# Odd layer's attention: the copies of transposed maps ahead of the exponentials, and low parts one step later

## The chip, the cores and the metric

The kernel runs on one core of a Trainium2 chip, as one launch. The metric is the device time of that launch in microseconds; three runs of the kernel before gave 1513.31, 1510.46 and 1513.28, a median of 1513.28. An engine here is one of five instruction streams that run side by side and wait for each other by semaphores: PE (TensorE: matmuls and transposes), DVE (VectorE), ACT (ScalarE), POOL (GpSimd) and SP (here only an issuer of DMAs). Each works through its own list strictly in order. Matmul results lie in PSUM, in banks of 512 f32 per partition; everything else lies in SBUF.

## The reference, cut

One inference step of a trunk with two layers over 128 context tokens (one group) and 256 latent tokens (the other), model width 1024. Each layer is: half SwiGLU, a mixer, half SwiGLU, each behind an RMS norm and an adaptive shift, scale and gate. The mixer of the even layer is differential attention beside a short convolution; that of the odd layer, which this change is about, is attention with 16 query heads on 4 key heads of 64, a window of 128 on either side among latent tokens, all context keys, and one sink logit per head:

```python
def _odd_mixer(h, w_in, w_out, qk_g, sink, rope=None, kv_ctx=None):
    q, k, v = jnp.split(h @ w_in, [...], axis=-1)
    q, k = _rms_norm(q, qk_g[0]), _rms_norm(k, qk_g[1])
    if kv_ctx is None:                  # context tokens: read context only
        o = _dense_sink_attention(q, k, v, sink)
    else:                               # latent tokens: window + cached context
        o = _window_sink_attention(_rope(q), _rope(k), v, k_ctx, v_ctx, sink)
    return o.reshape(b, s, ODD_OUT) @ w_out

# per block of 128 queries:
s_c = einsum("bqgrd,bcgd->bgrqc", qi, k_ctx) * scale
s_l = where(valid, einsum("bqgrd,bkgd->bgrqk", qi, ks) * scale, -inf)
p = softmax(concatenate([s_c, s_l, sink_column]))[..., :-1]
o = einsum(p[context], v_ctx) + einsum(p[window], vs)
```

## The kernel before, in words

**Products.** Large matrix products are done in f32 by parts: each operand is split into a rounded high part and the low part that is left, and a product is three matmuls, xh·wh + xl·wh + xh·wl (lines 178 to 180, names `proj`, `down`). Weights come by DMA (`raw`, on SP's queue), ACT writes their high part `wh` (line 80), and the DVE or POOL the low part `wl` (line 84). `refill_half` does half a weight tile of that at the end of each attention step.

**Steps.** The odd layer's attention is 24 steps (u, c, i): key head u of 4, chunk c of 2 (two query heads each), and i, a block of 128 queries: i = 0 the context block with 128 keys, i = 1 and 2 the two latent blocks with 384 keys. A step handles two heads, p = 0 and 1. `pipeline` runs the steps interleaved. In its round s it does, in this order of writing, which is the order of each engine's list:

- a(s), `scores`: PE multiplies queries and keys into two PSUM tiles `s` (line 1214) and, for i > 0, adds the mask by a matmul (1221). The DVE takes the maxima of both heads (1227, `omx`), multiplies them by the queries' scale (1229), forms the negative bias (1231, `ong`) and the sink's exponent (1235, `oes`). ACT computes the exponentials `e` of both heads with their sums (1239) and of the sink (1243).
- m(s-1), `normalised`: the DVE adds the sink to the sum (1247), takes the reciprocal (1248), and POOL multiplies both heads' maps by it (1249).
- fill(s): other work beside the attention. In the first half of the steps it is a piece of the query projection of a later head (PE, lines 178 to 180), with its norm (691 to 708, rsqrt on POOL at 189) and rotary embedding (718 to 722, DVE); from step 18 on, pieces of the output projection (`down`).
- b(s-3), `transposed`: PE transposes each map `e` in blocks of 128 into a PSUM tile `aT` (1259), and ACT copies that to SBUF as `at_sb` (1261).
- c(s-4), `attend`: PE multiplies the transposed maps with the values into the PSUM tile `oo` (1272). After i = 2 a chunk is finished: ACT writes its high part `gh` (1279), the DVE its low part `gl` (1280); they are the operands of the output projection.

So three rounds lie between a map's scores and its transposes, and four between scores and products.

**Buffers.** The PSUM tiles `aT`, `oo` and the running projection share four banks (tag "mm"); score tiles, norm rows and some small tiles share four others (tag "at"). A new tile takes the bank that was taken longest ago, and its first matmul waits until the last reader of the old tile is done. `at_sb` and two rotary temporaries share four SBUF buffers; maps have five.

The even layer's mixer uses `pipeline` as well, with its own functions.

Of the kernel before, what the change touches and what calls it, by code (L numbers as in the profile page):

```python
# [8 lines left out]
F32 = mybir.dt.float32  # L9
# [3 lines left out]
ALU = mybir.AluOpType  # L13
# [5 lines left out]
T = 384  # L19
# [39 lines left out]
class Weights:  # L59
# [82 lines left out]
    def refill(self):  # L142
        self.split(self.np + self.SPLIT)
# [10 lines left out]
class Kernel:  # L154
# [640 lines left out]
            nc.tensor.transpose(tp[:, h * P:(h + 1) * P], self.ck[:, h * P:(h + 1) * P], self.ident)  # L795
        nc.scalar.activation(out, tp[:, 0:n * P].rearrange("p (h t) -> p h t", h=n), AF.Copy)

    def pipeline(self, n, a, m, b, c, lag, fill, refill):

        for s in range(n + lag + 1):  # L800
            if s < n:
                a(s)
            if 0 <= s - 1 < n:
                m(s - 1)
            fill(s)
            if 0 <= s - lag < n:
                b(s - lag)
            if 0 <= s - lag - 1 < n:
                c(s - lag - 1)
            refill()  # L810
# [282 lines left out]
    def odd_mixer(self, l):  # L1093
        nc = self.nc
        okt = self.mix.tile([P, 4, 512], F32, tag="kt", name="okt")
        kt = [okt[:, i] for i in range(4)]
        vt = [self.mix.tile([P, 512], F32, tag=f"v{i}", name=f"ov{i}")[:, 0:256] for i in range(3)] + [self.cv]
# [4 lines left out]
        qs, rq = {}, {}  # L1102
# [83 lines left out]
        gs = [self.g_tiles(), self.g_tiles()]  # L1186
# [8 lines left out]
                next(out[0][2], None)  # L1195

        out, order = [], list(range(KC))
        self.pipeline(*self.odd_attention(qs, rq, kt, vt, gs), 3, fill, self.w.refill_half)
        self.out_projection(out[0], gs, order, self.mod_need(l, 5), (l, 2))

    def odd_attention(self, qs, rq, kt, vt, gs):

        nc = self.nc
        steps = [(u, c, i) for u in range(4) for c in range(2) for i in range(3)]

        def scores(u, c, i):

            keys = [kt[u // 2 + (0 if p == u % 2 else 2)] for p in range(2)]
            s = [self.ps("at", "s"), self.ps("at", "s")]
            n = 128 if i == 0 else 384  # L1210
            k0 = 384 if i == 0 else 0
            for p in range(2):
                hs = slice(64 * p, 64 * p + 64)
                nc.tensor.matmul(
                    s[p][:, 0:n], qs[u][hs, c, i * P:(i + 1) * P], keys[p][hs, k0:k0 + n],
                    start=True, stop=(i == 0),
                )
            if i:
                m0 = 256 if i == 1 else 128
                for p in range(2):  # L1220
                    nc.tensor.matmul(
                        s[p][:, m0:m0 + P], self.ident16, self.masks[i - 1], start=False, stop=True
                    )
            scale = rq[u][:, i, c]
            mx = self.small(2, "omx")
            for p in range(2):
                nc.vector.tensor_reduce(out=mx[:, p:p + 1], in_=s[p][:, 0:n], axis=AX.X, op=ALU.max)
            h0 = 4 * u + 2 * c
            nc.vector.tensor_tensor(out=mx, in0=mx, in1=scale, op=ALU.mult)
            ng = self.small(2, "ong")  # L1230
            nc.vector.scalar_tensor_tensor(
                out=ng, in0=mx, scalar=-1.0, in1=self.negsink[:, h0:h0 + 2], op0=ALU.mult, op1=ALU.min
            )
            es = self.small(2, "oes")
            nc.vector.tensor_tensor(out=es, in0=ng, in1=self.negsink[:, h0:h0 + 2], op=ALU.subtract)
            e = self.b3("e")
            rs = self.small(2, "ors")
            for p in range(2):
                nc.scalar.activation(
                    e[:, p, 0:n], s[p][:, 0:n], AF.Exp, bias=ng[:, p:p + 1], scale=scale[:, p:p + 1],  # L1240
                    accum_out=rs[:, p:p + 1],
                )
            nc.scalar.activation(es, es, AF.Exp)
            return e, n, rs, es

        def normalised(e, n, rs, es):
            nc.vector.tensor_tensor(out=rs, in0=rs, in1=es, op=ALU.add)
            nc.vector.reciprocal(rs, rs)
            nc.gpsimd.tensor_tensor(
                out=e[:, :, 0:n], in0=e[:, :, 0:n], in1=rs.unsqueeze(2).to_broadcast([P, 2, n]), op=ALU.mult  # L1250
            )
            return e, n

        def transposed(e, n):
            out = []
            for p in range(2):
                tp = self.ps("mm", "aT")
                for b in range(n // P):
                    nc.tensor.transpose(tp[:, b * P:(b + 1) * P], e[:, p, b * P:(b + 1) * P], self.ident)  # L1259
                at = self.a2("at_sb")[:, 0:n]  # L1260
                nc.scalar.activation(at, tp[:, 0:n], AF.Copy)
                out.append(at)
            return out, n

        def attend(u, c, i, ats, n):
            if i == 0:
                self.oo = self.ps("mm", "oo")
            vs = slice(u * HD, (u + 1) * HD)
            v = [vt[0]] if i == 0 else [vt[3], vt[1], vt[2]]
            for b in range(n // P):  # L1270
                for p in range(2):
                    nc.tensor.matmul(  # L1272
                        self.oo[64 * p:64 * p + 64, i * P:(i + 1) * P], v[b][:, vs],
                        ats[p][:, b * P:(b + 1) * P], start=(b == 0), stop=(b == n // P - 1),
                    )
            if i == 2:
                gh, gl = gs[u // 2]
                ch = 2 * (u % 2) + c
                nc.scalar.activation(gh[:, ch], self.oo[:, 0:T], AF.Copy)
                nc.vector.tensor_tensor(  # L1280
                    out=gl[:, ch], in0=self.oo[:, 0:T], in1=gh[:, ch].bitcast(F32), op=ALU.subtract
                )

        maps, ats = {}, {}

        def a(n):
            maps[n] = scores(*steps[n])

        def m(n):
            maps[n] = normalised(*maps[n])  # L1290

        def b(n):
            ats[n] = transposed(*maps.pop(n))

        def c(n):
            attend(*steps[n], *ats.pop(n))

        return len(steps), a, m, b, c


    def setup(self):
# [342 lines left out]
```

## Time and profile before

| | us |
|---|---|
| median of three runs | 1513.28 |
| lowest, highest | 1510.46, 1513.31 |
| the profiled execution | 1516.13 |
| its span in the trace | 1514.3 |
| from the first scores of the odd attention to the first `down` behind its last step | 1105.24 to 1189.94 |
| mean granted clock of TensorE, as a share of full speed | 0.993 |

The profile is of one execution and lists what each engine ran, with the time that it stood idle ahead of each group and the event that ended it. In a row of groups, x24 is the number of instructions; behind the bar stand their busy time in us, the mean of one in ns, and the idle time before them with its releasers. In a timeline, a row is start, duration, engine, line, operation, output <- inputs; the bracket is the idle time before it and its releaser. A window's row has busy times of five engines (with instruction counts), then the granted TensorE clock (PEclk, 1.00 is full), the share of the DMA engines and their rate. PEld is TensorE's weight load, which overlaps its matmuls.

### The profile page before, as it was taken

What the parts mean: (1) busy time and instruction counts of PE and PEld (TensorE: products, weight loads), DVE (VectorE), ACT (ScalarE), POOL (GpSimd) and SP (SyncE); (2) the same over time, 40 slices, a digit from 0 to 9 for tenths busy, and PEclk for the clock granted to TensorE, in tenths of its full rate; (3) what the DMA queues carried; (4) which work ended last, traced back from release to release, by engine and by line L of the source; (5) the groups of instructions that cost most, each with busy time, mean ns of one, the idle gap of its engine ahead of it and who ended that gap; (6) DMA issues with size and microseconds to landing.
All of it is one profiled execution on the core that took longest, in us unless ns stands there. A gap on an engine that the chain in (4) does not pass through costs nothing.

```text
span 1514.3 us, 22676 instructions
## 1 busy us (share of the span) xinstructions
PE 1479.7 (98%) x9082; PEld 1414.8 (93%) x9082; DVE 1047.3 (69%) x1670; ACT 658.1 (43%) x1235; POOL 149.3 (10%) x99
## 2 busy tenths in 40 slices
PE   6999999999999999999999999999998999999998
PEld 6999999999899999999999999999965799999998
DVE  3848799777777887878689777766786485344432
ACT  3633233465555632334464333425666564323322
POOL 1100000015322100000010000000454220000000
PEclk8999999999999999999999999999998999999999
DMA  9846887553323465866546667634330034344322
GB/s 349 279 159 216 253 266 234 181 168 112 112 86 118 145 209 187 256 219 204 157 153 212 215 199 245 218 110 152 114 99 29 5 112 142 109 137 142 110 79 76
DMA packets 192155, 248.61 MB, mean 164 GB/s; under 512 B 5845, under 2 KB 170290, under 8 KB 192050
## 3 DMA queue, kind: packets, MB, share of 16 engines
q1 hardware_dynamic: 190974, 245.79, 49.9%
q8 instruction: 71, 1.16, 0.3%
q10 hardware_dynamic: 1076, 1.38, 0.3%
q14 instruction: 34, 0.28, 0.1%
HBM read 244.26 MB, written 2.36 MB: 163 GB/s over the span
## 4 chain that ended last, share of the span: by engine, by line
PE 80%; DVE 10%; ACT 4%; issue 2%; DMA 2%; POOL 1%; ACTq 0%; DVEq 0%; POOLq 0%
PE proj L178 16%; PE proj L180 16%; PE proj L179 16%; PE down L178 8%; PE down L179 8%; PE down L180 8%; DVE macc L225 3%; DVE wl L84 2%; ACT wh L80 1%; DMA wm<-in_w_mod 1%; DVE acc L342 1%; PE m_sum L237 1%; PE oo L1272 1%; DVE x L347 1%; PE aT L1259 1%
## 5 line engine op out<-in xcount | busy, mean ns | idle before, releaser
L178 PE MATMUL proj<-xh,wh 128*128 128x384 f32 (+1 forms) x1648 | 562.8, 341 | 1.7 <-ACT xh L395 1.7
L180 PE MATMUL proj<-xh,wl 128*128 128x384 f32 (+1 forms) x1648 | 557.2, 338 | 0.9 <-DVE wl L84 0.9
L179 PE MATMUL proj<-xl,wh 128*128 128x384 f32 (+1 forms) x1648 | 556.4, 338 | 0.0
L84 DVE TENSOR_TENSOR wl<-raw,wh 128x1024 fp32r<-128x1024 f32 (+2 forms) x332 | 360.6, 1125 | 187.5 <-ACT wh L80 187.1
L80 ACT ACTIVATE wh<-raw 128x1024 fp32r<-128x1024 f32 x356 | 321.6, 952 | 138.8 <-PE down L179 109.3
L178 PEld LDWEIGHTS proj<-xh,wh 128*128 128x128 f32 x1648 | 310.6, 188 | 14.8 <-issue 6.8
L180 PEld LDWEIGHTS proj<-xh,wl 128*128 128x128 f32 x1648 | 311.1, 189 | 1.2 <-DVE wl L84 1.2
L179 PEld LDWEIGHTS proj<-xl,wh 128*128 128x128 f32 x1648 | 310.6, 188 | 0.0
L178 PE MATMUL down<-gh,wh 128*128 128x384 f32 x832 | 280.6, 337 | 0.4 <-ACT gh L642 0.4
L179 PE MATMUL down<-gl,wh 128*128 128x384 f32 x832 | 278.4, 335 | 0.5 <-DVE gl L643 0.5
L180 PE MATMUL down<-gh,wl 128*128 128x384 f32 x832 | 278.2, 334 | 0.0
L225 DVE SCALAR_TENSOR_TENSOR macc<-wm,cpad,macc 128x1024 f32<-128x1024 f32 x210 | 258.1, 1279 | 3.0 <-DMA wm<-in_w_mod 2.4
L642 ACT ACTIVATE gh<-gf 128x768 fp32r<-128x768 f32 x44 | 37.2, 846 | 291.9 <-DVE gf L632 287.5
L178 PEld LDWEIGHTS down<-gh,wh 128*128 128x128 f32 x832 | 156.3, 188 | 4.4 <-issue 3.6
L179 PEld LDWEIGHTS down<-gl,wh 128*128 128x128 f32 x832 | 156.4, 188 | 1.0 <-DVE gl L643 0.8
L180 PEld LDWEIGHTS down<-gh,wl 128*128 128x128 f32 x832 | 156.3, 188 | 0.0
L625 ACT ACTIVATE sg<-proj 128x384 f32<-128x384 f32 x78 | 37.5, 488 | 136.0 <-PE proj L180 136.0
L347 DVE SCALAR_TENSOR_TENSOR x<-down,m,x 128x128 f32<-128x128 f32 (+1 forms) x160 | 59.1, 411 | 49.5 <-PE down L180 48.7
L632 DVE TENSOR_TENSOR gf<-proj,sg 128x384 f32<-128x384 f32 x78 | 43.2, 554 | 70.2 <-PE proj L180 70.2
L84 POOL TENSOR_TENSOR wl<-raw,wh 128x1024 fp32r<-128x1024 f32 x24 | 61.4, 2560 | 107.3 <-ACT wh L80 95.4
L643 DVE TENSOR_TENSOR gl<-gf,gh 128x768 fp32r<-128x768 f32 x44 | 42.2, 959 | 40.1 <-ACT gh L642 40.1
L189 POOL TENSOR_TENSOR nr<-nv,neghalf 128x3 f32<-128x3 f32 x6 | 5.1, 851 | 570.6 <-DVE nv L415 570.6
(221 smaller groups left out, 1084.9 us busy)
## 6 DMA issues: line engine op xcount, KB each, us to landing
raw<-in_ffn_w SPq DMA_DIRECT2D x85, 1024.0 KB
wm<-in_w_mod SPq DMA_DIRECT2D x126, 512.0 KB
raw<-in_ffn_w SPq DMA_DIRECT2D x32, 768.0 KB
raw<-in_ffn_w SPq DMA_DIRECT2D x32, 640.0 KB
raw<-in_even_w_in SPq DMA_DIRECT2D x12, 1024.0 KB
raw<-in_odd_w_in SPq DMA_DIRECT2D x6, 1024.0 KB
raw<-in_even_w_out SPq DMA_DIRECT2D x4, 1024.0 KB
raw<-in_odd_w_out SPq DMA_DIRECT2D x4, 1024.0 KB
```

What stands on the lines that cost most here:

```text
L80: self.k.nc.scalar.activation(parts[0][:, a:b], raw[:, a:b], AF.Copy)
L84: engine.tensor_tensor(out=lo[:, a:b], in0=raw[:, a:b], in1=h[:, a:b].bitcast(F32), op=ALU.subtract)
L178: mm(out, w[0], x[0], start=first, stop=False)
L179: mm(out, w[0], x[1], start=False, stop=False)
L180: mm(out, w[1], x[0], start=False, stop=last)
L225: nc.vector.scalar_tensor_tensor(out=acc, in0=t, scalar=c, in1=acc, op0=ALU.mult, op1=ALU.add)
L237: self.nc.tensor.matmul(ps[32 * j:32 * j + 32, 0:256], c, v[:, j], start=first, stop=last)
L347: self.nc.vector.scalar_tensor_tensor(out=self.x[oc][:, a:b], in0=psum[:, a:b], scalar=gate[:, oc, g:g + 1], in1=self.x[oc][:, a:b], op0=A ...
L625: nc.scalar.activation(sg[c], out[:, 0:T], AF.Silu)
L632: nc.vector.tensor_tensor(out=gf[:, c], in0=out[:, 0:T], in1=sg[c], op=ALU.mult)
L642: nc.scalar.activation(gh, gf, AF.Copy)
L643: nc.vector.tensor_tensor(out=gl, in0=gf, in1=gh.bitcast(F32), op=ALU.subtract)
```

## The change

`scores` is cut in two: `scores` keeps the matmuls, and a new function `exponentials` has all behind them (maxima, scale, bias, exponentials). `pipeline` gets an optional argument e. With it, a round is: a(s), the score matmuls; b(s-3), transposes and copies; e(s), maxima and exponentials; m(s-1); fill(s); c(s-4); refill. Without it, as in the even layer, the round is what it was. The low part `gl` of a finished chunk is no longer written in `attend` but noted in a list, which `low_parts` works off at the end of the next m; for the last key head (u = 3) at once. Every operation of before is there once, with the same operands.

```diff
@@ -795,15 +795,19 @@
             nc.tensor.transpose(tp[:, h * P:(h + 1) * P], self.ck[:, h * P:(h + 1) * P], self.ident)
         nc.scalar.activation(out, tp[:, 0:n * P].rearrange("p (h t) -> p h t", h=n), AF.Copy)
 
-    def pipeline(self, n, a, m, b, c, lag, fill, refill):
+    def pipeline(self, n, a, m, b, c, lag, fill, refill, e=None):
 
         for s in range(n + lag + 1):
             if s < n:
                 a(s)
+            if e and 0 <= s - lag < n:
+                b(s - lag)
+            if e and s < n:
+                e(s)
             if 0 <= s - 1 < n:
                 m(s - 1)
             fill(s)
-            if 0 <= s - lag < n:
+            if not e and 0 <= s - lag < n:
                 b(s - lag)
             if 0 <= s - lag - 1 < n:
                 c(s - lag - 1)
@@ -1195,7 +1199,8 @@
                 next(out[0][2], None)
 
         out, order = [], list(range(KC))
-        self.pipeline(*self.odd_attention(qs, rq, kt, vt, gs), 3, fill, self.w.refill_half)
+        a, e, m, b, c = self.odd_attention(qs, rq, kt, vt, gs)
+        self.pipeline(24, a, m, b, c, 3, fill, self.w.refill_half, e)
         self.out_projection(out[0], gs, order, self.mod_need(l, 5), (l, 2))
 
     def odd_attention(self, qs, rq, kt, vt, gs):
@@ -1221,6 +1226,9 @@
                     nc.tensor.matmul(
                         s[p][:, m0:m0 + P], self.ident16, self.masks[i - 1], start=False, stop=True
                     )
+            return s, n
+
+        def exponentials(u, c, i, s, n):
             scale = rq[u][:, i, c]
             mx = self.small(2, "omx")
             for p in range(2):
@@ -1277,17 +1285,26 @@
                 gh, gl = gs[u // 2]
                 ch = 2 * (u % 2) + c
                 nc.scalar.activation(gh[:, ch], self.oo[:, 0:T], AF.Copy)
-                nc.vector.tensor_tensor(
-                    out=gl[:, ch], in0=self.oo[:, 0:T], in1=gh[:, ch].bitcast(F32), op=ALU.subtract
-                )
-
-        maps, ats = {}, {}
+                lows.append((gl[:, ch], self.oo[:, 0:T], gh[:, ch].bitcast(F32)))
+                if u == 3:
+                    low_parts()
+
+        def low_parts():
+            for out, psum, high in lows:
+                nc.vector.tensor_tensor(out=out, in0=psum, in1=high, op=ALU.subtract)
+            lows.clear()
+
+        maps, ats, lows = {}, {}, []
 
         def a(n):
             maps[n] = scores(*steps[n])
 
+        def e(n):
+            maps[n] = exponentials(*steps[n], *maps[n])
+
         def m(n):
             maps[n] = normalised(*maps[n])
+            low_parts()
 
         def b(n):
             ats[n] = transposed(*maps.pop(n))
@@ -1295,7 +1312,7 @@
         def c(n):
             attend(*steps[n], *ats.pop(n))
 
-        return len(steps), a, m, b, c
+        return a, e, m, b, c
 
 
     def setup(self):
```

The line numbers of the changed kernel are higher: scores 1219 and 1226, maxima 1235 to 1243, exponentials 1247 and 1251, sum, reciprocal and scaling 1255 to 1257, transposes 1267, copies 1269, products 1280, `gh` 1287, `gl` 1294.

What moves in the engines' lists shows at three places. ACT, rounds 12 and 13, before: `e` are a round's own exponentials, `at_sb` the copies of the round three earlier, `gh` the high part of the chunk finished four rounds earlier.

```order
L1239 ACTIVATE e,ors<-s,ong,orq_10570 128x128 x2
L1243 ACTIVATE oes<-oes 128x2
L1261 ACTIVATE at_sb<-aT 128x128 x2
L1279 ACTIVATE gh<-oo 128x384
L1239 ACTIVATE e,ors<-s,ong,orq_10570 128x384 x2
L1243 ACTIVATE oes<-oes 128x2
L1261 ACTIVATE at_sb<-aT 128x384 x2
```

and now:

```order
L1269 ACTIVATE at_sb<-aT 128x128 x2
L1247 ACTIVATE e,ors<-s,ong,orq_10582 128x128 x2
L1251 ACTIVATE oes<-oes 128x2
L1287 ACTIVATE gh<-oo 128x384
L1269 ACTIVATE at_sb<-aT 128x384 x2
L1247 ACTIVATE e,ors<-s,ong,orq_10582 128x384 x2
L1251 ACTIVATE oes<-oes 128x2
```

The copies of the transposed maps of steps 9 and 10 stood behind the exponentials of steps 12 and 13, and stand ahead of them now; `gh` stays behind the 128-key exponentials.

DVE, the end of round 12 and round 13, before: first sum and reciprocal of step 11, then the low part, the maxima of step 13 and what follows from them, sum and reciprocal of step 12, and the norm of a projection (`orq_v`).

```order
L1247 TENSOR_TENSOR ors<-ors,oes 128x2
L1248 RECIPROCAL ors<-ors 128x2
L1280 TENSOR_TENSOR gl<-oo,gh 128x384
L1227 TENSOR_REDUCE omx<-s 128x1 x2
L1229 TENSOR_TENSOR omx<-omx,orq_10570 128x2
L1231 SCALAR_TENSOR_TENSOR ong<-omx,negsink 128x2
L1235 TENSOR_TENSOR oes<-ong,negsink 128x2
L1247 TENSOR_TENSOR ors<-ors,oes 128x2
L1248 RECIPROCAL ors<-ors 128x2
L708 TENSOR_SCALAR orq_v<-cols 128x12
```

and now:

```order
L1255 TENSOR_TENSOR ors<-ors,oes 128x2
L1256 RECIPROCAL ors<-ors 128x2
L1235 TENSOR_REDUCE omx<-s 128x1 x2
L1237 TENSOR_TENSOR omx<-omx,orq_10582 128x2
L1239 SCALAR_TENSOR_TENSOR ong<-omx,negsink 128x2
L1243 TENSOR_TENSOR oes<-ong,negsink 128x2
L1255 TENSOR_TENSOR ors<-ors,oes 128x2
L1256 RECIPROCAL ors<-ors 128x2
L1294 TENSOR_TENSOR gl<-oo,gh 128x384
L708 TENSOR_SCALAR orq_v<-cols 128x12
```

The low part `gl` went from ahead of the maxima of step 13 to behind the reciprocal of step 12. Nothing else moved.

PE, round 9 (a 128-key step with a projection piece), before: scores of step 9, six projection matmuls, transposes of step 6, products of step 5.

```order
L1214 MATMUL s<-okt,oq 128x128 x2
L178 MATMUL proj<-xh,wh 128x384
L179 MATMUL proj<-xl,wh 128x384
L180 MATMUL proj<-xh,wl 128x384
L178 MATMUL proj<-xh,wh 128x384
L179 MATMUL proj<-xl,wh 128x384
L180 MATMUL proj<-xh,wl 128x384
L1259 MATMUL aT<-con,e 128x128 x2
L1272 MATMUL oo<-at_sb,v_4446 64x128 x2
L1272 MATMUL oo<-at_sb,ov_9815 64x128 x2
L1272 MATMUL oo<-at_sb,ov_9816 64x128 x2
```

and now:

```order
L1219 MATMUL s<-okt,oq 128x128 x2
L1267 MATMUL aT<-con,e 128x128 x2
L178 MATMUL proj<-xh,wh 128x384
L179 MATMUL proj<-xl,wh 128x384
L180 MATMUL proj<-xh,wl 128x384
L178 MATMUL proj<-xh,wh 128x384
L179 MATMUL proj<-xl,wh 128x384
L180 MATMUL proj<-xh,wl 128x384
L1280 MATMUL oo<-at_sb,v_4446 64x128 x2
L1280 MATMUL oo<-at_sb,ov_9815 64x128 x2
L1280 MATMUL oo<-at_sb,ov_9816 64x128 x2
```

The transposes went from behind the fill's matmuls to straight behind the scores; the products stay behind the fill. POOL's list is in the same order as before.

## The prediction

> **What bounds the kernel now.** I read the page first, its span and its busy times.
>
> ```profile
> span 1514.3 us, 22676 instructions
> PE 1479.7 (98%) x9082; PEld 1414.8 (93%) x9082; DVE 1047.3 (69%) x1670; ACT 658.1 (43%) x1235; POOL 149.3 (10%) x99
> ```
>
> The kernel as a whole hangs on TensorE. A reordering on ACT and DVE can win only where PE stands or runs at half clock. So the second view is the table of windows. I cut the odd layer's attention at the score matmuls: seven stretches (steps 0 to 5, then three steps each, the last 21 to 23), then what follows it; the last two rows are chosen for their clock.
>
> ```profile
> core 0: us, PE busy (x) PEld busy (x) DVE busy (x) ACT busy (x) POOL busy (x), PEclk, DMA share, GB/s
> 1105.24:1126.79 21.55, 19.92 (x120) 13.45 (x120) 20.23 (x51) 11.68 (x37) 12.00 (x7) 1.00 0.15 49
> 1126.79:1137.53 10.74, 10.41 (x79) 7.42 (x77) 7.60 (x30) 7.18 (x24) 5.74 (x4) 1.00 0.30 99
> 1137.53:1148.00 10.47, 10.14 (x76) 6.44 (x74) 7.23 (x28) 8.37 (x26) 4.23 (x4) 1.00 0.01 2
> 1148.00:1161.67 13.67, 10.62 (x64) 6.32 (x62) 8.95 (x27) 8.48 (x28) 8.10 (x6) 0.79 0.23 77
> 1161.67:1171.23 9.56, 7.62 (x61) 4.78 (x59) 5.08 (x22) 6.76 (x27) 4.30 (x4) 0.86 0.01 3
> 1171.23:1180.47 9.24, 9.09 (x71) 6.36 (x69) 5.18 (x22) 5.53 (x20) 2.52 (x3) 0.90 0.00 0
> 1180.47:1189.94 9.47, 7.38 (x64) 4.59 (x62) 5.19 (x22) 7.02 (x27) 4.09 (x4) 1.00 0.05 16
> 1189.94:1514.30 324.36, 318.17 (x1856) 315.07 (x1854) 146.70 (x222) 116.50 (x195) 14.66 (x10) 1.00 0.33 106
> 1156.10:1162.40 6.30, 5.40 (x27) 3.44 (x27) 2.50 (x13) 4.23 (x14) 4.38 (x4) 0.50 0.51 166
> 1170.00:1172.90 2.90, 2.90 (x19) 2.34 (x18) 0.77 (x4) 1.72 (x7) 1.07 (x1) 0.50 0.03 6
> ```
>
> Call the seven stretches A to G. In A the DVE is busy for 94%. In B and C PE is busy for 97%. In D, E and G PE stands for 3.05, 1.94 and 2.09. In D to F two pieces run at a granted clock of 0.50. Behind 1189.94 PE is busy for 98%: an earlier end of the attention passes on whole. Third, the groups of the attention alone, with what ended the idle time ahead of each:
>
> ```profile
> L1259 PE MATMUL aT<-con,e 128*128 128x128 f32 x98 | 16.6, 292 | 5.8 <-ACT at_sb L1261 5.3 <-POOL e L1249 0.3
> ...
> L1229 DVE TENSOR_TENSOR omx<-omx,orq 128x2 f32<-128x2 f32 x24 | 11.1, 463 | 0.9
> ...
> L189 POOL TENSOR_TENSOR orq<-orq_v,neghalf 128x12 f32<-128x12 f32 x3 | 7.7, 2574 | 4.1 <-PE s L1214 4.1
> L84 POOL TENSOR_TENSOR wl<-raw,wh 128x1024 fp32r<-128x1024 f32 x3 | 7.1, 2356 | 0.0
> ...
> L1280 DVE TENSOR_TENSOR gl<-oo,gh 128x384 fp32r<-128x384 f32 x6 | 3.3, 558 | 10.0 <-ACT gh L1279 10.0
> ```
>
> L1259 and L1280 are the two waits that the change takes on. PE stands 5.3 us at transposes (aT) that need the bank of a map which ACT has not copied yet (at_sb). The DVE stands 10.0 us at the low parts (gl) until ACT has written gh, six times. The timeline of steps 22 and 23 shows how one leads to the other.
>
> ```profile
> 1183.68 0.92 PE L1214 MATMUL s<-okt,oq 64*128 64x384 f32 x4
> ...
> 1184.32 0.56 DVE L1280 TENSOR_TENSOR gl<-oo,gh 128x384 fp32r<-128x384 f32 x1 [1.97 <-ACT gh L1279]
> ...
> 1184.65 0.82 PE L1259 MATMUL aT<-con,e 128*128 128x128 f32 x6
> 1184.79 1.02 DVE L1227 TENSOR_REDUCE omx<-s 128x1 f32<-128x384 f32 x2
> ...
> 1185.77 0.92 PE L1214 MATMUL s<-okt,oq 64*128 64x384 f32 x4
> ...
> 1186.32 0.67 ACT L1239 ACTIVATE e<-s,ong,orq 128x384 f32<-128x384 f32 x1 [2.04 <-DVE ong L1231]
> 1186.51 0.17 DVE L1248 RECIPROCAL ors<-ors 128x2 f32<-128x2 f32 x1
> ...
> 1186.84 0.61 POOL L1249 TENSOR_TENSOR e<-e,ors 128x256 f32<-128x256 f32 x1 [2.86 <-DVE ors L1248]
> ...
> 1187.73 0.86 ACT L1261 ACTIVATE at_sb<-aT 128x384 f32<-128x384 f32 x2
> ...
> 1188.35 0.85 PE L1259 MATMUL aT<-con,e 128*128 128x128 f32 x6 [1.45 <-ACT at_sb L1261]
> ...
> 1189.94 0.44 PE L178 MATMUL down<-gh,wh 128*128 128x384 f32 x1
> ```
>
> gl holds back the maxima of step 22 to 1184.79, these the exponentials to 1186.32, and behind both exponentials stand the copies of maps that PE had finished by 1185.47: they start at 1187.73. PE, one step on, waits for them until 1188.35. One late gl costs one standing PE.
>
> **The change part by part.** Nothing is added or removed: per step two copies, two exponentials and six transposes stay, and six gl of 0.56 stay. No DMA moves past another; POOL's and SP's queues keep their order.
>
> (1) What PE needs by itself. Step 22 runs without a gap: 1183.68 to 1185.77 is 2.09. Step 23 is its scores (1183.68 to 1184.65, 0.97) and its transposes and products (1188.35 to 1189.94, 1.59): 2.56. A 128-key step has those 1.59 less two thirds of the 0.82 of transposes, and some 0.4 of scores: 1.45, an estimate. Three steps: 6.1.
>
> (2) What ACT needs: its busy 6.76 in E and 7.02 in G.
>
> (3) What DVE and POOL need, now that gl stands behind the reciprocal. From the start of the maxima to the reciprocal's end a 384-key step takes 1.89 (1184.79 to 1186.68). A 128-key step reduces a third as much: about 1.36, an estimate. Two and one: 5.14, with gl 5.70. On top comes a lock:
>
> ```profile
> 1138.09 1.47 POOL L1249 TENSOR_TENSOR e<-e,ors 128x768 f32<-128x768 f32 x1 [3.04 <-DVE ors L1248]
> ...
> 1138.57 1.00 DVE L1229 TENSOR_TENSOR omx<-omx,orq 128x2 f32<-128x2 f32 x1
> ```
>
> A scale multiply (L1229) of 0.16 lasts 1.00, to POOL's end at 1139.56. With the maxima straight behind the reciprocal, POOL's 1.47 starts 0.16 behind it and ends at 1.63; the multiply would start at 1.05, or 0.53 in a 128-key step: holds of 0.58 and 1.10 per three steps, none under the 0.61 form. 5.70 + 1.68 = **7.4 per three steps**, above ACT's and PE's sums: DVE and POOL would be the bound of the steps without projections.
>
> [...]
>
> (4) The sum by stretches. **A: 0**, down to the 1.3 that the DVE idles; it is full of DVE work (query projections, rope, wl) in nearly the same order. **B and C**: PE idles 0.33 in each, and six projection matmuls take 1.14 a step (rows below), so PE's own three steps are 6.1 + 3.4 = 9.5, against 10.74 and 10.47.
>
> ```profile
> 1141.69 0.56 DVE L1280 TENSOR_TENSOR gl<-oo,gh 128x384 fp32r<-128x384 f32 x1 [1.45 <-ACT gh L1279]
> ...
> 1141.89 0.42 PE L178 MATMUL proj<-xh,wh 128*128 128x384 f32 x1
> ...
> 1142.17 1.01 DVE L1227 TENSOR_REDUCE omx<-s 128x1 f32<-128x384 f32 x2
> ...
> 1143.03 0.71 PE L1259 MATMUL aT<-con,e 128*128 128x128 f32 x5
> ```
>
> Between 0 and -2.2; the maxima that gl holds have their scores hardly earlier (1142.08), so nearer the 0.66 of idle: -1.1. **D**:
>
> ```profile
> 1151.95 0.28 PE L1221 MATMUL s<-m,ident 128*128 128x128 bf16 x2
> ...
> 1152.44 1.47 POOL L1249 TENSOR_TENSOR e<-e,ors 128x768 f32<-128x768 f32 x1 [3.65 <-ACT e L1239]
> ...
> 1153.86 2.34 POOL L84 TENSOR_TENSOR wl<-raw,wh 128x1024 fp32r<-128x1024 f32 x1
> 1154.19 1.01 DVE L1227 TENSOR_REDUCE omx<-s 128x1 f32<-128x384 f32 x2
> ...
> 1157.00 1.64 PE L1214 MATMUL s<-okt,oq 64*128 64x384 f32 x2 [2.06 <-DVE orq_v L708]
> ```
>
> Step 13's scores are there at 1152.23; its maxima start at 1154.19, behind gl, and its multiply then meets wl on POOL. Without gl ahead the maxima start 1.9 earlier, the multiply is held only by the 1.47 (to 1153.91), and the exponential, 1.53 behind the start of the maxima as in step 22 and held some 0.6 more, starts at about 1154.4. Step 14's second score matmul, which the new program lets wait for that exponential's first half (0.67) in place of L708, comes at about 1155.1: -1.9. Behind the 2.06 of standing the clock was 0.50 from 1156.10 to 1162.40; its part in D, some 5.0 of work, would take half: -2.5. One such spell may stay somewhere after a gap of about 2 us, and the shortest shown (2.90, all busy) costs 1.45. D: -3.0, between 0 and -4.4. **E** from 9.56 to 7.4: -2.2 (between 0 and -2.8, ACT's sum). **F** has an out-projection piece of some 0.52 a step (half of a projection piece's 1.14, an estimate): PE's 6.1 + 1.6 = 7.7 against 9.24: -1.5 (its half clock included). **G** from 9.47 to 7.4: -2.1 (between 0 and -2.5). The moved transposes now stand ahead of the projections on PE; they cost nothing while POOL is ahead of them (rival 3).
>
> (5) Waits that the new program has and the old one not, as its order and banks show. The products of a step that opens a chunk take the bank of a transpose of their own step and wait for its copy; ACT does that next (0.43 for half of the 0.86), beside PE's projections, or inside the 1.3 that PE has to spare in E to G: 0, at most 0.4 in three steps. The transposes of steps 8, 11 and 20 wait for the gl of the step before, which stands behind a reciprocal that ended before these scores: 0. Rope's shuffle on the DVE in steps 7 and 11 waits for the products of its own step on PE, and the next maxima queue behind it: 0 to 1 each, a step's projections; I take 0, since these maxima wait for PE too. Together 0, at worst +3.
>
> Sum: 0 - 1.1 - 3.0 - 2.2 - 1.5 - 2.1 = **-9.9**, ends +3 and -14.7. From the profiled 1516.13 that is 1506.2; this run lies 2.85 over the median 1513.28, so 1503.4 by the median.
>
> [...]
>
> **The rivals.** *Rival 1, half the gain.* If the multiply of step 13 slips under POOL's wl all the same (2.34), and if the three unfilled stretches fall only to 8.5 since ACT's copies, exponentials and the holds don't fit into each other, D gives -1.5 and E to G -1.1, -0.7, -1.0; with -0.7 in B and C -5.0: 1508.3. For it: L1229 loses 7.3 us already (11.1 less 24 of 0.16). Against it: step 13's own times.
>
> *Rival 2, no change.* Where gl went, the next wait is as long: in 1141.69 it is worth 0.1, since the scores come no earlier. If that holds in E to G too (scores waiting for the banks of the exponentials of two steps before), only D's 1.9 stays: 1511.4. For it: B and C. Against: in G the scores of step 22 were there well before 1184.79. That the change doesn't do what it says is excluded by the order shown above.
>
> *Rival 3, slower.* The copies of step s-3 now stand ahead of the exponentials of step s, and the transposes ahead of the projections. If POOL has not scaled map s-3 when PE reaches its transposes, PE stands with the projections behind it, and the exponentials queue behind the copies. POOL ends 2.05 + 1.47 behind the start of step s-2's maxima, these 1.12 behind its scores; the transposes come 0.97 behind the scores of s. The slack is two steps less 3.7: 3.3 at B's 3.5 a step, 1.2 at 7.4 per three. A POOL wl (2.36) or the norms' rsqrt (2.57, both from the groups above) alone stays within B's 3.3; the two together ahead of one scaling overdraw it by 1.6, which is the point from which it decides. There are three of each: three pairs lose 4.9 and bring three spells of half clock at 1.45, 9.2, against the 5.8 that E to G still give: +3.4, 1516.7. For it: in D wl and an rsqrt stand close, with one scaling of 0.61 between them. Against it: all six lie in A to D, whose steps are the longest, and POOL idles there.
>
> **How the numbers follow.** Forecast 1503.4, chance 0.66, own range 1499 to 1507; rival 1 1508.3, 0.16; rival 2 1511.4, 0.12; rival 3 1516.7, 0.06. A measurement here tells 0.2% (3.0 us) from no change. So faster 0.82, same 0.12, slower 0.06. The low end 1498.5 is the median less all the largest gains together; the high end 1510.5 takes in rival 1 and leaves out 2 and 3.
>
> **What would show it.** Right: the 10.0 before gl gone or under 1; at_sb no longer the releaser of aT; no standing of PE over 1.5 from 1148 on; E and G at 7 to 7.8; the attention shorter by about 10 and the rest unchanged. Wrong: PE waiting at aT for POOL's e; exponentials waiting for aT; L1229's group over 16 us; a new spell of half clock; or stretches E to G with the old length and their waits put down to score matmuls.

## The result, and the profile after

The changed kernel takes 1504.85 us (median of 5 runs, 1504.54 to 1506.85) against 1513.28: a ratio of 0.9948, 95% interval 0.9936 to 0.9960, some 8 us. Its profiled execution took 1506.42, with a span of 1504.6.

The windows of the changed kernel, cut at the same score matmuls as before, the seventh at the end of step 23's round (us from the start; then length, busy times of PE, PEld, DVE, ACT and POOL with counts, granted clock, share and rate of the DMA engines):

```profile
1104.34:1125.55 21.21, 19.63 (x120) 13.30 (x120) 19.78 (x49) 12.44 (x39) 11.82 (x7) 1.00 0.15 51
1125.55:1136.24 10.69, 9.86 (x78) 7.19 (x76) 7.57 (x33) 7.90 (x25) 5.94 (x5) 1.00 0.31 100
1136.24:1145.34 9.10, 9.10 (x76) 6.08 (x74) 5.61 (x22) 7.62 (x25) 3.67 (x4) 1.00 0.01 3
1145.34:1159.11 13.77, 9.57 (x63) 5.73 (x61) 11.02 (x29) 8.46 (x27) 8.31 (x6) 0.88 0.23 76
1159.11:1165.34 6.23, 6.23 (x61) 4.00 (x59) 4.52 (x19) 5.62 (x22) 3.19 (x3) 1.00 0.02 4
1165.34:1173.44 8.10, 8.07 (x71) 5.53 (x69) 6.85 (x26) 7.33 (x25) 3.64 (x4) 1.00 0.00 0
1173.44:1180.79 7.35, 6.98 (x63) 4.60 (x62) 4.95 (x19) 6.16 (x23) 3.46 (x3) 1.00 0.07 21
1180.79:1504.60 323.81, 318.07 (x1856) 314.83 (x1854) 147.13 (x225) 117.12 (x197) 15.64 (x10) 1.00 0.33 106
```

| stretch (steps) | before | after | measured | forecast |
|---|---|---|---|---|
| A (0 to 5) | 21.55 | 21.21 | -0.3 | 0 |
| B, C (6 to 11) | 21.21 | 19.79 | -1.4 | -1.1 |
| D (12 to 14) | 13.67 | 13.77 | +0.1 | -3.0 |
| E (15 to 17) | 9.56 | 6.23 | -3.3 | -2.2 |
| F (18 to 20) | 9.24 | 8.10 | -1.1 | -1.5 |
| G (21 to 23) | 9.47 | 7.35 | -2.1 | -2.1 |
| sum | 84.70 | 76.45 | -8.2 | -9.9 |

Of the span's 9.7, 8.2 lie in the attention and 0.6 behind it; 0.9 lie ahead of the first scores, where the programs are alike, and so are not the change's. In E PE is busy for the whole 6.23, and in C too. In E and F 2.4 of the gain is that PE's own work, of the same number of matmuls, no longer runs partly at half clock (busy 6.23 against 7.62, and 8.07 against 9.09). D is the exception: PE stands for 4.2 of its 13.77, at a mean clock of 0.88. The groups of the attention, with the idle time ahead of each and its releaser:

```profile
L1267 PE MATMUL aT<-con,e 128*128 128x128 f32 x100 | 15.7, 287 | 0.0
L1269 ACT ACTIVATE at_sb<-aT 128x384 f32<-128x384 f32 (+1 forms) x42 | 15.5, 421 | 5.6 <-PE aT L1267 4.3 <-PE oo L1280 0.6 <-ACT onk L1187 0.4
L1237 DVE TENSOR_TENSOR omx<-omx,orq 128x2 f32<-128x2 f32 x24 | 11.3, 473 | 0.9
L1239 DVE SCALAR_TENSOR_TENSOR ong<-omx,negsink 128x2 f32<-128x2 f32 x24 | 6.0, 249 | 0.8
L1294 DVE TENSOR_TENSOR gl<-oo,gh 128x384 fp32r<-128x384 f32 x6 | 3.2, 537 | 0.0
```

Both waits are gone: PE's 5.3 at aT for at_sb, the DVE's 10.0 at gl. In their place ACT waits 4.3 for transposes; none of PE's waits in the attention follows from one of these. One line is longer: ong (L1239), 24 of 0.16 before, has 6.0 in all, 2.1 too much. The timeline of step 13 shows where:

```profile
1150.07 1.00 DVE L1235 TENSOR_REDUCE omx<-s 128x1 f32<-128x384 f32 x2
...
1150.33 1.47 POOL L1257 TENSOR_TENSOR e<-e,ors 128x768 f32<-128x768 f32 x1 [3.64 <-ACT e L1247]
...
1151.11 0.70 DVE L1237 TENSOR_TENSOR omx<-omx,orq 128x2 f32<-128x2 f32 x1
...
1151.75 2.34 POOL L84 TENSOR_TENSOR wl<-raw,wh 128x1024 fp32r<-128x1024 f32 x1
1151.84 2.27 DVE L1239 SCALAR_TENSOR_TENSOR ong<-omx,negsink 128x2 f32<-128x2 f32 x1
...
1154.20 0.67 ACT L1247 ACTIVATE e<-s,ong,orq 128x384 f32<-128x384 f32 x1 [2.20 <-DVE ong L1239]
...
1155.02 1.41 PE L1219 MATMUL s<-okt,oq 64*128 64x384 f32 x2 [3.03 <-ACT e L1247]
```

The multiply is held to the end of POOL's scaling (it ends at 1151.81, POOL at 1151.80). POOL goes straight on to wl, and ong, the next on the DVE, ends with wl (1154.11 and 1154.09). The exponentials and PE's second score matmul of step 14 wait for it: 3.03 us, and then half clock (0.50 from 1155.28 to 1158.69).

### The profile page after: what moved, and what is told of

The parts are those of the page before. It is cut to its first block, busy times and chain, and to the rows that moved or that the text cites. A ratio compares the mean times of both kernels' runs of the same rounds, so it can differ in the third digit from the quotient of the medians.

```text
span 1504.6 us, 22708 instructions
## 1 busy us (share of the span) xinstructions
PE 1473.6 (98%) x9082; PEld 1411.2 (94%) x9082; DVE 1048.2 (70%) x1670; ACT 659.4 (44%) x1235; POOL 149.4 (10%) x99
## 4 chain that ended last, share of the span: by engine, by line
PE 82%; DVE 9%; ACT 3%; issue 2%; DMA 2%; POOL 1%; ACTq 0%; DVEq 0%; POOLq 0%
PE proj L178 16%; PE proj L180 16%; PE proj L179 16%; PE down L178 9%; PE down L179 8%; PE down L180 8%; DVE macc L225 3%; DVE wl L84 2%; ACT wh L80 1%; DMA wm<-in_w_mod 1%; PE oo L1280 1%; PE s L1219 1%; DVE acc L342 1%; PE m_sum L237 1%; PE aT L1267 1%
```

## The experiments

Every kernel was timed in several rounds beside the kernel before on the same chip; ratios are to that kernel. Stretches are named as above.

**The parts apart.** Only the low parts one step later; the round is the old one:

```diff
-        self.pipeline(24, a, m, b, c, 3, fill, self.w.refill_half, e)
+        def whole(n):
+            a(n)
+            e(n)
+        self.pipeline(24, whole, m, b, c, 3, fill, self.w.refill_half)
```

> The low parts go one step later as in the change, the copies stay behind the exponentials and the transposes behind the fill. Theory A (one chain: a late gl makes late maxima, late exponentials and so late copies, on which PE stands): most of the gain comes already here, 5 to 7 us under the kernel before; the 10.0 us of idle DVE ahead of gl fall under 1, the 5.3 us of PE idle on at_sb under 2. Rival B (the place of the copies is what counts): at most 2 us under before, PE still idle 4 to 5 us on at_sb. In stretch D (steps 12 to 14) both expect a lock of the DVE under POOL's wl and a length of 13 to 14.

Measured: 1.0010 (1.0001 to 1.0018): no gain. Theory A had 5 to 7 us and falls; B's "at most 2 us" holds for the time. PE's wait for copies came out between the two, at 2.4 (A had under 2, B 4 to 5). PE's waits in the attention of this kernel (total, times, longest; the first three):

```profile
PE oo L1284 <- DVE gl L1298: 4.5, 4, 1.8
PE aT L1271 <- ACT at_sb L1273: 2.4, 4, 0.8
PE s L1223 <- ACT e L1251: 2.2, 1, 2.2
```

The DVE no longer waits ahead of gl, but PE does behind it. In the built program the products of the next chunk take the PSUM bank of the finished one, and so wait for the low part that reads it, now one step later. In step 19:

```profile
1173.82 0.54 DVE L1298 TENSOR_TENSOR gl<-oo,gh 128x384 fp32r<-128x384 f32 x1
...
1174.50 0.44 PE L1284 MATMUL oo<-at_sb,ov 128*64 128x128 f32 x4 [1.24 <-DVE gl L1298]
```

The copies are less late than before (2.4 against 5.3), but still behind the exponentials. What PE saves there it loses to gl.

Only the new round, that is, transposes and copies ahead of the exponentials; gl stays where it was:

```diff
-                if u == 3:
-                    low_parts()
+                low_parts()
```

> The new round with the copies ahead of the exponentials, but gl in its old place, ahead of the next maxima. Theory A: 2 to 4 us under before, since gl still waits for gh behind the exponentials and holds the next maxima (8 to 10 us of idle DVE ahead of gl); PE no longer stands on at_sb but on the exponentials of two steps before. Rival B: 6 to 8 us under before, nearly all of the change. If the two parts add, this and the run with the low parts alone give 8.4 together.

Measured: 0.9966 (0.9954 to 0.9978), some 5 us of the 8, between the two theories. The DVE still stands 8.7 us ahead of gl. PE's waits, three of them:

```profile
PE s L1219 <- DVE orq_v L708: 2.9, 1, 2.9
...
PE oo L1280 <- DVE gl L1293: 0.6, 1, 0.6
PE aT L1267 <- ACT at_sb L1269: 0.4, 1, 0.4
```

At aT PE hardly stands any more (0.4 against 5.3); the 2.9 are the wait in stretch D that the kernel before has too (2.06). The parts don't add: nothing and 5 alone, 8 together. With the transposes and copies ahead, banks come free in another order: in the built program of the changed kernel no chunk takes the bank of the chunk before it, and in its trace no product waits for gl.

Only PE's part of the new round: transposes ahead of the fill, copies behind the exponentials.

```diff
             if e and 0 <= s - lag < n:
                 b(s - lag)
             if e and s < n:
                 e(s)
+            if e and 0 <= s - lag < n:
+                b(s - lag, True)
```

(`b` without True now does the transposes alone, with True the copies.)

> The changed kernel, with only the ACT copies put back behind the exponentials of their round: the transposes stay ahead of the fill on PE, gl one step late. Theory A (what the change takes away is the wait of PE for copies that stand behind the exponentials in ACT's list): the wait of transposes or products for at_sb comes back with 4 to 8 us, more than the 5.3 of before since the transposes come earlier, and the time is 4 us or more above the changed kernel. Rival B (it is PE's own order, transposes ahead of the projections, that counts): within 1 us of the changed kernel.

Measured: 1.0039 (1.0026 to 1.0051), 6 us slower than the kernel before. PE's waits:

```profile
PE aT L1269 <- ACT at_sb L1277: 4.7, 5, 1.9
PE oo L1288 <- DVE gl L1302: 4.6, 4, 1.8
PE aT L1269 <- POOL e L1259: 4.2, 4, 2.1
```

Theory A's reading, that the copies' place on ACT is what frees PE from the copies, holds: the wait for them is back at 4.7. Rival B falls. Of the 15 us over the changed kernel the copies are only a part: PE also waits 4.6 for gl and 4.2 for POOL's scaling, the mechanism of rival 3. Transposes ahead of the fill harm when the copies aren't ahead too.

**Stretch D.** The one wl on POOL behind the scaling of step 11 goes to the DVE:

```diff
+        rounds = iter(range(28))
+        def refill():
+            light, self.light = self.light, next(rounds) != 12 and self.light
+            self.w.refill_half()
+            self.light = light
-        self.pipeline(24, a, m, b, c, 3, fill, self.w.refill_half, e)
+        self.pipeline(24, a, m, b, c, 3, fill, refill, e)
```

> The changed kernel, with the one wl that POOL does between the scalings of steps 11 and 12 given to the DVE (1.22 us there, ahead of the maxima of step 13). Theory C (the stretch of steps 12 to 14 didn't get shorter because POOL's 2.34 us of wl lock the DVE's ong of step 13, and PE then stands 3.03 us and runs at half clock): ong takes 0.16, the exponentials of step 13 start about 1.4 earlier, PE's standing falls to about 1.6 and the half clock goes: 1.5 to 3 us under the changed kernel. Rival D (PE waits there for something else, and the lock hides under it): within 0.5 us of the changed kernel.

Measured: 0.9946 (0.9934 to 0.9958), the time of the changed kernel, so the expected 1.5 to 3 us failed and the time is rival D's. As in theory C, no ong is long now (24 in 3.9 us) and PE's standing fell from 3.03 to 1.74; but the half clock stayed and was longer. Here and below the first row is the 3.4 us ahead of it:

```profile
1149.60:1153.00 3.40, 1.60 (x9) 0.75 (x9) 3.26 (x10) 2.49 (x9) 2.28 (x1) 1.00 0.24 76
1153.00:1159.80 6.80, 6.49 (x33) 4.21 (x34) 3.05 (x15) 3.64 (x14) 4.31 (x3) 0.50 0.33 116
```

The maxima in PSUM, so that multiply and ong have one operand in SBUF:

```diff
-            mx = self.small(2, "omx")
+            mx = s[0][:, 384:386]
```

> The changed kernel, with the maxima kept in two unused columns of the score tile in PSUM, so that the scale multiply and ong have one operand in SBUF instead of two. Theory C (the holds are a lock between a DVE operation with two SBUF operands and a POOL one): no multiply and no ong longer than 0.3 us, though the sink's exponent behind them still is held; stretch D 3 to 4 us shorter, the whole 3 to 5 us under the changed kernel. Rival (the holds are of the DVE as a whole while POOL runs, or come from the semaphores): the groups of multiply and ong stay at 11 and 6 us and the time is that of the changed kernel or above it.

Measured: 0.9937 (0.9925 to 0.9950), median 1504.47. The lock is as theory C has it: all 24 multiplies take 168 to 169 ns and all ong 159 to 160, and the hold passes to the operations behind them that have two SBUF operands (the sink's exponent L1243, up to 1.60 us, and the sum L1255, up to 2.31), off PE's path. PE's standing for step 13 is 0.72 in place of 3.03. Yet the time hardly moved, and the expected 3 to 5 us failed. Again the clock:

```profile
1148.50:1151.90 3.40, 2.08 (x14) 0.99 (x12) 3.04 (x12) 2.59 (x9) 2.04 (x2) 0.99 0.00 0
1151.90:1158.70 6.80, 6.47 (x33) 4.18 (x35) 5.01 (x15) 3.88 (x14) 5.99 (x4) 0.50 0.47 154
```

So the spell needs neither one long standing nor a gap of about 2 us: in the 3.4 us ahead of this one no pause was longer than 0.93.

**The clock.** The spells of half clock so far lie on a grid. In the profile before they last 10.24 us (from 19.32), 6.82 (from 1155.96) and 3.41 (from 1169.61), with 1126.38 and 6.81 at full clock between them; in that of the changed kernel 10.23 (from 18.63) and 3.41 (from 1155.28), with 1126.40 between. These are 1, 2, 3 and 330 times 3.4133, within 0.02.

The changed kernel again, for its spells:

> The changed kernel once more, beside the others on the same chip: 8 us under before. If the half clock behind step 13 is a matter of where PE's idle time falls in a free running window, its spell in this profile is 0, about 3.4 or about 6.8 us long, not 3.4 again of necessity, and the times of the runs fall into groups some 1.7 or 3 us apart with the mean clock.

Measured: 0.9944 (0.9930 to 0.9957), median 1505.00. The first profile had a spell of 3.4 (second row, behind the 3.4 us ahead of it):

```profile
1151.87:1155.28 3.41, 0.38 (x2) 0.27 (x2) 3.17 (x6) 1.21 (x4) 2.75 (x2) 1.00 0.02 2
1155.28:1158.70 3.42, 3.42 (x18) 2.04 (x19) 1.75 (x7) 1.49 (x6) 2.31 (x2) 0.50 0.93 305
```

The same program, with the same standing (3.04), now has one of 6.8, and it starts 7.79 behind the start of D, not 9.94 as in the first profile, so its start isn't tied to a place in the program:

```profile
1150.65:1157.45 6.80, 4.91 (x24) 3.18 (x26) 3.67 (x13) 3.56 (x10) 4.74 (x4) 0.50 0.49 154
```

D and E together take 20.67 here (14.34 and 6.33), 20.00 in the first profile. Beside it, with spells of the same 6.8, wl on the DVE gives 20.08 (13.04 and 7.04) and the maxima in PSUM 19.43 (12.46 and 6.97). By these profiles, one of each kernel, the lock is thus worth about 1.2; the first comparisons had hidden it behind spells of different length. The times were not in the clear groups that had been expected (1504.62 to 1506.32).

Spare transposes, results unused, to fill PE's pauses in round 13, on top of the maxima in PSUM; in `b` and `c`, all into columns 384 to 511 of the round's last aT:

```diff
+            for _ in range(8 if n == 10 else 0):
+                self.spare()
...
             attend(*steps[n], *ats.pop(n))
+            for _ in range(7 if n == 9 else 0):
+                self.spare()
```

> The kernel with the maxima in PSUM, and 15 spare transposes (0.13 us each by the rows, results unused) on PE in round 13, 8 behind that round's transposes and 7 behind its products, where PE stood 0.93 and 0.72 us. Theory E (the half clock comes from these gaps together, short as each is): the clock stays at 1.00 from 1140 to 1190, the stretch of steps 12 to 17 is 2.5 to 3 us shorter than with the 6.8 us spell, and the time is at most that of the fastest runs with the maxima in PSUM (1502.3), some 2 us under their median. Rival F (the spells come whatever PE does there): half clock stays and the time is 0 to 0.5 us above that kernel.

Measured: 0.9951 (0.9938 to 0.9964), a median of 1506.93, worse than without them: the spare transposes waited for the copy of the tile that they wrote beside, a new wait.

```profile
PE aT L1271 <- ACT at_sb L1269: 2.6, 1, 2.6
```

So the pause was made longer and not filled. Yet the clock of this profile stays at 1.00 from 1142 to 1190, as theory E had expected of filled pauses:

```profile
1148.00:1150.00 2.00, 0.31 (x3) 0.07 (x1) 1.76 (x8) 1.36 (x7) 0.81 (x1) 1.00 0.00 0
1150.00:1152.00 2.00, 1.09 (x9) 0.93 (x10) 1.90 (x5) 2.00 (x7) 2.00 (x2) 1.00 0.00 0
```

PE is busy for 1.40 of these 4.00 and no half clock follows. This speaks against theory E's reason. Despite the new wait, D and E take 18.71 (12.32 and 6.39), 0.7 less than with the maxima in PSUM alone; 2.5 to 3 had been expected.

Without the wait: 7 ahead of the round's last copy, 7 into unused columns of `oo` behind the products.

```diff
+                for _ in range(spare if p else 0):
+                    nc.tensor.transpose(tp[:, 384:512], e[:, 1, 0:P], self.ident)
                 at = self.a2("at_sb")[:, 0:n]
...
             attend(*steps[n], *ats.pop(n))
+            for _ in range(7 if n == 9 else 0):
+                nc.tensor.transpose(self.oo[:, 384:512], last[0][0][:, 1, 0:P], self.ident)
```

> Maxima in PSUM and 14 spare transposes on PE in round 13 (7 with that round's transposes ahead of their copies, 7 behind its products), put so that none waits for a copy, unlike in the run before. Theory E (PE's idle share ahead of the end of one of the clock's windows brings the half clock): no half clock between 1140 and 1190 in the profile, steps 12 to 17 in 16 to 17 us against 19.4 with the maxima in PSUM alone, nearly all runs in one group at 1502 to 1503, 11 us under before. Rival F (spells come whatever PE does): a spell of 3.4 or 6.8 us stays and the time is 1504 to 1505.

Measured: 0.9916 (0.9903 to 0.9930), median 1502.31, the best of all, though the interval overlaps that of the maxima in PSUM alone. The same places of this kernel:

```profile
1148.72:1152.12 3.40, 3.25 (x27) 2.52 (x26) 3.04 (x12) 2.59 (x9) 2.04 (x2) 1.00 0.00 0
1144.66:1154.98 10.32, 9.48 (x77) 6.34 (x75) 9.62 (x23) 7.97 (x26) 5.98 (x5) 1.00 0.01 1
1154.98:1162.32 7.34, 6.93 (x60) 4.28 (x58) 6.51 (x24) 5.74 (x22) 5.62 (x4) 1.00 0.45 145
```

PE is busy for 3.25 of the 3.40 in which it had been busy for 2.08, and no half clock follows. D and E take 17.66, 1.8 less than without the spare work (16 to 17 had been expected). The runs reach from 1500.81 to 1503.78, wider than expected.

The same in the changed kernel itself, with 5 and 22 spare transposes and the lock left in:

> The changed kernel with 27 spare transposes in round 13 (5 with the transposes, 22 behind the products, some 2.9 us inside PE's 3.04 us of standing), nothing else. Theory E: the standing for the exponentials of step 13 falls under 0.5 us without the end of the stretch coming earlier by itself, the half clock goes, and the time falls 1.5 to 3 us under the changed kernel's median, to 1502 to 1503.5. Rival F: half clock stays, time that of the changed kernel, 1505.

Measured: 0.9930 (0.9918 to 0.9942), median 1504.56, lowest 1502.34, so the time fell less than expected: the intervals of this and of the changed kernel overlap. The profile, which is of the lowest run, is as theory E has it:

```profile
1142.27:1154.49 12.22, 11.10 (x91) 7.76 (x89) 10.63 (x26) 7.86 (x25) 7.92 (x5) 1.00 0.19 58
1154.49:1160.71 6.22, 6.22 (x61) 3.99 (x59) 5.83 (x20) 5.54 (x21) 3.60 (x4) 1.00 0.18 59
```

D and E take 18.44 at full clock, against 20.00 and 20.67 with spells of 3.4 and 6.8. Spare work and no lock together, in the run before, take 17.66. All three profiles with spare transposes are free of half clock in the attention, and all eight without them have it in stretch D. That the spare work takes it away is thus likely; that it does so by making PE busier is not shown, since the first of the three had its long pause as well.

## Why the prediction was right, and where its terms were not

The measured 1504.85 is 1.4 over the forecast of 1503.4 and within its own range of 1499 to 1507. That the sum came so near is in part luck: D came out 3.1 us above its term, E 1.1 below, and of what lies between the two profiles 1.5 us fell away outside the attention, where the forecast had nothing.

**The waits taken away: right.** Over the same six chunks 10.0 and 5.3 both fell to 0.0, and the attention is 8.2 shorter.

**"One late gl costs one standing PE": wrong as a chain.** gl alone moved away does shorten PE's wait for copies (5.3 to 2.4), as the chain has it, but gives no time: the wait comes back on PE as a bank that isn't free (4.5). The copies' place on ACT is what PE's waits at aT hang on: 5 of the 8 us come with the new round alone, transposes ahead without the copies lose 6, and gl's move is worth the other 3 only together with the round. The prediction went through the bank waits of the whole program and not of its halves, and for the whole it was right: products wait 0.4 for a copy, once, and nothing waits for gl.

**Term D (-3.0): wrong, +0.1.** The step that failed is that "the multiply is held only by the 1.47" and the exponential then starts. The hold of the multiply came as computed (0.54 over its own 0.16, against some 0.6), but ong behind it has two SBUF operands as well, and the wl that POOL starts at the end of its scaling took it for 2.27. It is rival 1's mechanism one instruction on, and with PE's 3.03 the forecast's sign "no standing of PE over 1.5" failed. Without this lock and without the half clock D takes 10.32, 3.35 less than before.

**Term E (-2.2): too small, -3.3.** The step that failed is the bound of 7.4 per three steps, which put the maxima straight behind the reciprocal. There they don't stand; they wait for PE's scores:

```profile
1159.64 0.49 DVE L1235 TENSOR_REDUCE omx<-s 128x1 f32<-128x128 f32 x2 [1.06 <-PE s L1219]
...
1161.16 1.47 POOL L1257 TENSOR_TENSOR e<-e,ors 128x768 f32<-128x768 f32 x1 [0.94 <-ACT e L1247]
...
1161.83 1.02 DVE L1235 TENSOR_REDUCE omx<-s 128x1 f32<-128x384 f32 x2 [0.84 <-PE s L1226]
...
1162.88 0.16 DVE L1237 TENSOR_TENSOR omx<-omx,orq 128x2 f32<-128x2 f32 x1
```

While the DVE waits, POOL gets on: its 1.47 ends at 1162.63, before the multiply at 1162.88, and nothing is held. The bound is PE's own work, 6.1 by the prediction and 6.23 measured. A hold that would arise only if the DVE were the bound can't make it the bound while PE is slower.

**Terms A, B and C, F, G: right** within 0.4 each. G's 7.35 is near the forecast 7.4 for another reason: PE is busy for 6.98 of it, with an out-projection piece that the forecast had left out.

**The half clock: one spell stayed, as assumed**, but the reason given (a gap of about 2 us) is refuted both ways: a spell came with no pause over 0.93 ahead of it, and none came behind one of 2.60. The spells of before are also longer than the windows that the prediction read them from: 6.8 and 3.4 us (from 1155.96 and from 1169.61) in place of 6.30 and 2.90, so its 1.45 for the shortest should be 1.7. **Rival 3** was rightly small: after the change no transpose waits for POOL. Its mechanism is real, though: 4.2 us in the run with transposes ahead and copies behind.

## What to carry to other kernels

Look for the copy that stands behind an engine's next big operation although its input has long been ready: moved ahead, it frees the banks that the matmul engine waits for (here PE's 5.3 us at aT went to 0.0). A release that is moved later must be followed to who takes that buffer next (gl alone moved later brought PE a new wait of 4.5), and two edits that share a pool of buffers are to be judged together. A resource's bound counts only if nothing slower paces it: work out the slowest engine's time first, and let the others' holds arise at that pace.

## What the runs showed of the hardware

**Half clock comes in pieces of about 3.4 us; what brings it stays open.** The spells and what lies between them in the profiles before and after the change are 1, 2, 3 and 330 times 3.4133 us, by the figures given ahead of the second run of the changed kernel. Spells in the attention were 3.4 or 6.8 long, in the same program too. The 3.4 us ahead of a spell had PE busy for 0.38 (the change), 1.60 (wl on the DVE), 2.08 (maxima in PSUM) or even 2.45 (low parts only):

```profile
1150.60:1154.00 3.40, 2.45 (x15) 1.37 (x15) 3.26 (x8) 1.80 (x8) 2.65 (x2) 1.00 0.00 0
```

With 3.25 there was none, but neither was there one with PE busy for 1.40 of 4.00 (the first run with spare transposes). So busy time by the records alone doesn't decide. Nor does it take a stretch in which PE does nothing: in the 3.40 ahead of the maxima's spell it was busy for 2.08 by the records. In the profiles of this kernel, transposes that compute nothing bought 1.6 to 2.2 us in stretches D and E (18.44 against 20.00 and 20.67; 17.66 against 19.43); the times of the runs don't set this apart from their scatter.

**With one operand in PSUM the DVE's multiply and ong were no longer held by POOL.** The same multiply took up to 2.20 us with two SBUF operands beside a POOL operation (the changed kernel), and never over 0.17 with one (the maxima in PSUM; the one at 1150.85 stood beside POOL's 1.47 from 1149.86); the scalar-tensor-tensor ong went from at most 2.27 to 0.16. Operations behind them that kept two SBUF operands took over the hold: the sum, up to 2.31, ended at 1153.64 with POOL's wl at 1153.62.
